# Weight rows moved within 256 bytes, high and low parts interleaved, tokens streamed in either direction

## The chip, the cores and the metric

One NeuronCore of a Trainium2 chip runs the whole program. The metric is the device time of one execution in microseconds. The kernel before was timed twice, and one further execution was taken by the hardware profiler.

## What is computed

One layer of a decoder on 256 prompt tokens and 8 sample tokens, with everything in fp32. The bulk of the arithmetic is matrix products of the 264 tokens with weights; `D_MODEL` is 2048 and the feed-forward width is 5632:

```python
xn = rmsnorm(x, g_mix)
z = xn @ w_in                                   # all inputs of the two mixers
...
x = x + jnp.concatenate([y_rg, y_ml], axis=-1) @ w_out
xq = (rmsnorm(x, g_xa) @ w_xa_q).reshape(B, L, XA_HEADS, XA_DH)
s = jnp.einsum('blhd,bmhd->bhlm', xq, mk.astype(dt)).astype(jnp.float32) * (XA_DH ** -0.5)
...
x = x + o @ w_xa_o
xf = rmsnorm(x, g_ffn)
x = x + (jax.nn.silu(xf @ w_ffn_gate) * (xf @ w_ffn_up)) @ w_ffn_down
```

Between them stand an RG-LRU recurrence, an mLSTM, and attention to 256 memory tokens, whose keys and values (`w_xa_k`, `w_xa_v`) are projected from `mem_prompt`.

## The kernel before

Activations lie with features on the 128 partitions and the 264 tokens along the row. The program is a list, `steps`, written out in order: 41 of `w_in`, 16 of `w_out`, 16 of `w_q`, 32 of `w_k` and `w_v` by turns of four, 16 of `w_o`, then the feed-forward part as three parts of gate, up and down. One step makes one block of 128 output features (or, for `w_v`, adds to a block of 512). Its weights, up to 128x2048, come as two halves of 128x1024 into `raw` (`load_piece`, five buffers, issued by SyncE).

To keep fp32 precision at the fast matmul rate every operand is split into a high and a low part, both of type `float32r`: ScalarE copies the high part out, VectorE subtracts it from the original for the low part. `mm3` then makes three matmuls of each chunk of 128 input features: high by high, high by low, low by high. An ordinary step of 16 chunks so has 48 matmuls. Each loads 128x128 weights as the stationary operand and streams 264 columns of tokens as the moving one, and all 48 add into one PSUM bank.

`split_half` splits the weights of step `i + 1` while step `i` is on TensorE, into `w` tiles (four buffers of 128x2176 elements). In an ordinary step a chunk takes a row of 264 elements there, 128 high and 128 low ones one behind the other, and unused room; `wrows` cuts the rows out, beginning at element `WO`:

```python
WO, WW = 48, 8 * N + 64
...
w = w[:, WO: WO + 8 * N].rearrange("p (c n) -> p c n", n=N)
return w[:, :, 0: P], w[:, :, P: 2 * P]
```

A row of 264 elements is 1056 bytes, so each chunk begins 32 bytes further on, counted modulo 256. The token tiles (`HL`, `Arr`) have the same pitch of 264 elements, four chunks to a tile, and odd tiles begin 32 elements in, so the tokens' chunks move on by 32 bytes in the same way. All `w` and `B` buffers begin at a multiple of 256 bytes. With `WO = 48`, weights and tokens of one chunk therefore always stand 192 bytes apart modulo 256.

The steps of `w_k` and `w_v` are called `wide`: their halves lie in one piece each, the high part at element 0 and the low part at 1088 (both at byte 0 modulo 256). In `w_k` (`pe_k`) the weights are stationary and 512 or 256 token columns move; in `w_v` (`pe_v`) the tokens are stationary and 512 weight columns move. `proj` makes the ordinary steps but for those of `w_o` (`pe_o`), the gates (`pe_if`) and the first four steps (`pe_first`). The first four take their chunks in another order, four outputs at once.

Side work (the recurrences, the norms, attention) runs from generators that `pump` advances between steps within time that the program estimates for ScalarE and VectorE.

Of the kernel before, what the change touches and what calls it, by code (L numbers as in the profile page):

```python
# [17 lines left out]
P = 128  # L18
# [4 lines left out]
N = T + NS  # L23
# [57 lines left out]
def layer_kernel(ctx: ExitStack, tc, xT, memT, vec, wrg, w_in, w_out, w_q, w_k, w_v, w_o,  # L81
# [18 lines left out]
    def nm(s):  # L100
        uid[0] += 1
        return f"{s}_{uid[0]}"
# [16 lines left out]
    WO, WW = 48, 8 * N + 64  # L119
# [29 lines left out]
    steps = []  # L149
    LD, LS = 3, 1  # L150

    raws, splits, wide = {}, {}, set()
# [15 lines left out]
    def split_half(i, h):  # L168
        if i >= len(steps):
            return  # L170
        if steps[i][2] is pe_if:
            if h == 0:
                split_gates(i)
            return
        if i < 4:
            split_first(i, h)
            return
        nch = min(8, steps[i][1] // P - 8 * h)
        w = sb.tile([P, WW], F32R, tag="w", bufs=4, name=nm("w"))
        if i in wide:  # L180
            wh, wl = w[:, 0: 1024], w[:, 1088: 2112]
            with tc.high_priority():
                act.activation(wh, raws[i][h], AF.Copy)
                dve.tensor_sub(wl, raws[i][h], wh.bitcast(F32))
            splits[i, h] = (wh, wl)
            return
        wh, wl = wrows(w, i)
        r = raws[i][h].rearrange("p (c m) -> p c m", m=P)
        with tc.high_priority():
            st["split"] = act.activation(wh[:, :nch], r[:, :nch], AF.Copy)  # L190
            dve.tensor_sub(wl[:, :nch], r[:, :nch], wh[:, :nch].bitcast(F32))
        splits[i, h] = (wh, wl)
# [9 lines left out]
    def split_first(i, h):  # L202

        wh, wl = wrows(sb.tile([P, WW], F32R, tag="w", bufs=4, name=nm("w")), i)
        r = raws[i][h].rearrange("p (c m) -> p c m", m=P)
        with tc.high_priority(), in_order():
            for c in range(2):
                x, k = 4 * i + 2 * h + c, slice(4 * c, 4 * c + 4)
                split(*xn(x), xres[:, x, :], V("g_mix", x))
                st["split"] = act.activation(wh[:, k], r[:, k], AF.Copy)  # L210
                dve.tensor_sub(wl[:, k], r[:, k], wh[:, k].bitcast(F32))
        splits[i, h] = (wh, wl)

    def wrows(w, i):

        w = w[:, WO: WO + 8 * N].rearrange("p (c n) -> p c n", n=N)
        return w[:, :, 0: P], w[:, :, P: 2 * P]

    class W:
        def __init__(self, i):  # L220
# [11 lines left out]
    def mm3(ps, a, b, start, stop):  # L232
        ah, al = a
        bh, bl = b
        pe.matmul(ps, ah, bh, start=start, stop=False)
        pe.matmul(ps, ah, bl, start=False, stop=False)
        pe.matmul(ps, al, bh, start=False, stop=stop)
# [50 lines left out]
    def bank(tag="mm"):  # L288
        return psm.tile([P, 512], F32, tag=tag, bufs=4, name=nm(tag))
# [266 lines left out]
    def split_gates(i):  # L556

        for h in range(2):
            w = wrows(sb.tile([P, WW], F32R, tag="w", bufs=4, name=nm("w")), i)[0]
            x = raws[i][h].rearrange("p (c m) -> p c m", m=P)  # L560
            with tc.high_priority():
                act.activation(w[:, :, 0:64], x[:, :, 0:64], AF.Copy)
                dve.tensor_sub(w[:, :, 64:128], x[:, :, 0:64], w[:, :, 0:64].bitcast(F32))
            splits[i, h] = w
# [303 lines left out]
    def proj(src, rhs, evac, cols=2048, n=N, need=()):  # L868

        def f(i):  # L870
            ps = bank()
            w = W(i)
            nch = cols // P
            for c in range(nch):
                mm3(ps[:, :n], w(c), rhs(c), c == 0, c == nch - 1)
            return ps
        steps.append((src, cols, f, evac, need))

# [411 lines left out]
    with tc.high_priority(), in_order():  # L1290
        act.dma_start(vecs[:, 0:16], vec[:, 0:16])
        load_x(act, 1, 2)
        load_x(act, 2, 4)
        act.activation(warm_act, ones[:, 0:1], AF.Square)
        split_half(0, 0)
        split_half(0, 1)

    pend = []
    for i, (src, cols, pef, evf, need) in enumerate(steps):
# [13 lines left out]
        now = pe.clock  # L1313
        dve.clock, act.clock = max(dve.clock, now), max(act.clock, now)
        split_half(i + LS, 0)
        if i + LS < len(steps) and steps[i + LS][1] > 1024:
            split_half(i + LS, 1)
        ps = pef(i)
# [133 lines left out]
```

## Time and profile before

| | us |
|---|---|
| timed runs | 1550.17 and 1552.97, median 1551.57 |
| span of the profiled execution | 1548.1 |
| what lies around the span, by the two timed runs | 2.1 to 4.9 |
| TensorE, matmuls busy | 1533.5 (99%) |
| TensorE, weight loads busy | 1500.4 (97%) |
| VectorE busy | 1055.5 (68%) |
| ScalarE busy | 784.0 (51%) |
| GpSimd busy | 123.7 (8%) |
| mean DMA rate over the span | 211 GB/s |

PE is TensorE's matmul side and PEld its weight loads, which run beside the matmuls. Matmuls are pipelined: a row's duration is longer than the distance from its start to the next one's start, and it is the distance that adds up to the span. Nearly all engine work is issued through one helper, line 60, so the groups tell instructions apart by the tiles that they write and read: `mm<-B,w` are projection matmuls (token tiles `B`, weights `w`), `w<-raw` the splitting of weights.

### The profile page before, as it was taken

The numbers are of one execution on the slowest core, as the hardware profiler recorded it, in microseconds if no ns is written. First come the engines' busy times: TensorE is split into PE (matmuls) and PEld (weight loads), VectorE is DVE, ScalarE is ACT, GpSimd is POOL, SyncE is SP. The second block draws the span as 40 slices with busy tenths as digits, with TensorE's granted clock in tenths as the row PEclk, the third lists the DMA queues.
The fourth block names the chain that finished last, engine by engine and source line by source line (L and its number), as shares of the span: only waits on it lengthen the run. The fifth ranks groups of instructions, "written<-read, shape, count | busy, mean of one in ns | idle before, by whom it ended". The sixth has DMA issues, their size and how long they took to land.

```text
span 1548.1 us, 30188 instructions
## 1 busy us (share of the span) xinstructions
PE 1533.5 (99%) x12098; PEld 1500.4 (97%) x12098; DVE 1055.5 (68%) x2026; ACT 784.0 (51%) x1255; POOL 123.7 (8%) x190
## 2 busy tenths in 40 slices
PE   9999999999999999999999999999999999999997
PEld 9999999999999888899999999999999999999997
DVE  7886888796699989876665555445555545555554
ACT  7565775665455656555444444333444433444463
POOL 0001210000134333310000000000000000000000
PEclk9999999999999999999999999999999999999999
DMA  9556984547789887855555555555555555555563
GB/s 301 187 164 204 309 288 171 193 158 259 251 294 356 320 296 252 309 181 180 187 177 181 186 181 188 181 185 183 183 185 181 186 183 186 180 188 178 163 181 107
DMA packets 99757, 326.01 MB, mean 211 GB/s; under 512 B 10945, under 2 KB 19825, under 8 KB 99617
## 3 DMA queue, kind: packets, MB, share of 16 engines
q1 hardware_dynamic: 83472, 269.57, 52.1%
q0 software_dynamic: 15136, 53.16, 9.7%
q8 instruction: 94, 1.54, 0.4%
q10 hardware_dynamic: 1008, 1.36, 0.3%
q14 instruction: 47, 0.38, 0.1%
HBM read 312.78 MB, written 11.28 MB: 209 GB/s over the span
## 4 chain that ended last, share of the span: by engine, by line
PE 96%; DVE 2%; ACT 1%; DMA 0%; issue 0%; SPq 0%; DVEq 0%; ACTq 0%
PE mm L60 90%; PE ax L60 6%; DVE B L60 1%; ACT B L60 0%; DVE w L60 0%; DMA raw<-w_in 0%; ACT w L60 0%; ACT L60 0%; DVE xres L60 0%; DVE c L60 0%; ACT rstd L60 0%; SPq L1278 0%; DVE acc_x L60 0%; DVEq L1429 0%; ACT t L60 0%
## 5 line engine op out<-in xcount | busy, mean ns | idle before, releaser
L60 PE MATMUL mm<-B,w 128*128 128x264 f32 (+1 forms) x10960 | 1365.3, 285 | 4.1 <-DVE w L60 2.4
L60 PEld LDWEIGHTS mm<-B,w 128*128 128x128 f32 x10960 | 1338.6, 188 | 16.4 <-DVE w L60 2.8
L60 ACT ACTIVATE w<-raw 128x1024 fp32r<-128x1024 f32 (+1 forms) x522 | 537.9, 1031 | 654.6 <-PE mm L60 447.3
L60 DVE TENSOR_TENSOR w<-raw,w 128x1024 fp32r<-128x1024 f32 (+1 forms) x522 | 623.1, 1195 | 357.0 <-ACT w L60 356.0
L60 PE MATMUL mm<-w,B 128*128 128x512 f32 x384 | 91.0, 391 | 0.0
L60 PEld LDWEIGHTS mm<-w,B 128*128 128x128 f32 x384 | 70.7, 188 | 14.3
L60 DVE TENSOR_TENSOR t<-mm,rstd 128x264 f32<-128x264 f32 x104 | 44.8, 431 | 44.2 <-PE mm L60 43.5
L1344 POOL TENSOR_TENSOR B<-B,rstd 128x264 f32<-128x264 f32 x4 | 2.8, 736 | 855.5 <-ACT rstd L60 855.5
L60 DVE TENSOR_TENSOR xres<-xres,mm 128x264 f32<-128x264 f32 (+1 forms) x81 | 34.2, 423 | 38.9 <-PE mm L60 38.9
L60 DVE SCALAR_TENSOR_TENSOR B<-B,dw 128x256 f32<-128x256 f32 x128 | 55.6, 488 | 3.9 <-ACT dw L60 3.9
L60 DVE SCALAR_TENSOR_TENSOR dw<-B,qsm,dw 128x256 f32<-128x256 f32 x96 | 49.6, 525 | 0.4
L60 PE MATMUL ax<-B,B 128*128 128x256 f32 (+3 forms) x288 | 48.1, 308 | 0.0
L60 PEld LDWEIGHTS ax<-B,B 128*128 128x128 f32 x288 | 40.8, 190 | 3.2 <-ACT w L60 0.3
L1031 POOL TENSOR_TENSOR ds<-dw,ds 128x256 fp32r<-128x256 f32 x32 | 34.6, 1085 | 108.1 <-ACT ds L60 108.1
L60 ACT ACTIVATE B<-xres,vecs 128x264 fp32r<-128x264 f32 (+1 forms) x64 | 32.1, 502 | 1.5 <-DVE xres L60 1.0
L60 ACT ACTIVATE t<-xres 128x264 f32<-128x264 f32 (+2 forms) x61 | 24.0, 410 | 15.2 <-DVE xres L60 15.2
L1020 POOL DMA_DIRECT2D B<-kcT x32 | 17.3, 542 | 140.1 <-DVE B L60 131.0
L60 ACT ACTIVATE B<-t 128x264 fp32r<-128x264 f32 (+1 forms) x60 | 24.2, 409 | 4.6 <-DVE t L60 4.3
L60 DVE TENSOR_TENSOR acc_x<-acc_x,t 128x264 f32<-128x264 f32 x59 | 25.1, 426 | 1.0 <-ACT t L60 0.5
L60 DVE SCALAR_TENSOR_TENSOR B<-xres,vecs,B 128x264 fp32r<-128x264 f32 x48 | 23.4, 487 | 3.1 <-ACT B L60 3.1
L60 ACT ACTIVATE t<-t 128x264 f32<-128x264 f32 (+1 forms) x61 | 24.8, 406 | 1.3 <-DVE t L60 1.2
L60 ACT ACTIVATE dw<-B,qsm 128x256 f32<-128x256 f32 x32 | 16.2, 507 | 17.4 <-DVE B L60 10.7
(152 smaller groups left out, 666.9 us busy)
## 6 DMA issues: line engine op xcount, KB each, us to landing
raw<-w_gu SPq DMA_DIRECT2D x176, 512.0 KB, 3.5
raw<-w_d SPq DMA_DIRECT2D x80, 512.0 KB, 3.5
raw<-w_in SPq DMA_DIRECT2D x74, 512.0 KB, 4.6
raw<-w_out SPq DMA_DIRECT2D x32, 512.0 KB, 4.0
B<-kcT POOLq DMA_DIRECT2D x32, 512.0 KB, 8.1
raw<-w_q SPq DMA_DIRECT2D x32, 512.0 KB, 3.7
B<-vcT POOLq DMA_DIRECT2D x32, 512.0 KB, 8.5
raw<-w_k SPq DMA_DIRECT2D x32, 512.0 KB, 6.8
```

What stands on the lines that cost most here:

```text
L60: return f(*a, **k)
L1020: pool_e.dma_start(kc, kcT[h, b])
L1031: pool_e.tensor_sub(ws[:, 1], acc, ws[:, 0].bitcast(F32))
L1344: e.tensor_mul(st["y"](c), st["y"](c), r)
```

## The change

The place of the weights, their layout and the direction of the token stream become functions of the step. `placed(i)` gives three values for an ordinary step that is the `j`-th of its kind, counted from step 4 without the gates and the wide steps: the first element, `4 * (j // 4 % 16)`, which is a multiple of 16 bytes from 0 to 240; whether the high and low parts lie side by side (odd `j`); and whether the tokens are streamed backwards (`j % 4` of 2 or 3). The first four steps and the gates keep what they had.

Side by side means that element `2m` of a row is the high part of weight `m` and element `2m + 1` its low part, so ScalarE and VectorE write, and TensorE loads, with a step of two elements. Backwards means that the moving operand and the PSUM output are both read and written from the last column to the first, which leaves each token's sum at its own place. `pe_o` takes place and layout from `wrows` but always streams forwards. In the wide steps the first element becomes `4 * ((i - 4) % 16)`.

```diff
         w = sb.tile([P, WW], F32R, tag="w", bufs=4, name=nm("w"))
         if i in wide:
-            wh, wl = w[:, 0: 1024], w[:, 1088: 2112]
+            o = 4 * ((i - 4) % 16)
+            wh, wl = w[:, o: o + 1024], w[:, 1088 + o: 2112 + o]
...
     def wrows(w, i):
 
-        w = w[:, WO: WO + 8 * N].rearrange("p (c n) -> p c n", n=N)
+        o, side_by_side, _ = placed(i)
+        w = w[:, o: o + 8 * N].rearrange("p (c n) -> p c n", n=N)
+        if side_by_side:
+            w = w[:, :, 0: 2 * P].rearrange("p c (m j) -> p c j m", j=2)
+            return w[:, :, 0], w[:, :, 1]
         return w[:, :, 0: P], w[:, :, P: 2 * P]
+
+    def placed(i):
+
+        if i < 4 or steps[i][2] is pe_if:
+            return WO, False, False
+        j = len([k for k in range(4, i) if k not in wide and steps[k][2] is not pe_if])
+        return 4 * (j // 4 % 16), j % 2 == 1, j % 4 > 1
...
             ps = bank()
             w = W(i)
             nch = cols // P
+            back = slice(None, None, -1 if placed(i)[2] else 1)
             for c in range(nch):
-                mm3(ps[:, :n], w(c), rhs(c), c == 0, c == nch - 1)
+                mm3(ps[:, :n][:, back], w(c), [v[:, back] for v in rhs(c)], c == 0, c == nch - 1)
             return ps
```

## The prediction

> **What bounds the kernel now.** I read the busy shares and the forty slices first, then the chain that ended last.
>
> ```profile
> span 1548.1 us, 30188 instructions
> PE 1533.5 (99%) x12098; PEld 1500.4 (97%) x12098; DVE 1055.5 (68%) x2026; ACT 784.0 (51%) x1255; POOL 123.7 (8%) x190
> ...
> PE   9999999999999999999999999999999999999997
> ...
> PEclk9999999999999999999999999999999999999999
> ...
> PE 96%; DVE 2%; ACT 1%; DMA 0%; issue 0%; SPq 0%; DVEq 0%; ACTq 0%
> PE mm L60 90%; PE ax L60 6%; DVE B L60 1%; ACT B L60 0%; DVE w L60 0%; DMA raw<-w_in 0%; ACT w L60 0%; ACT L60 0%; DVE xres L60 0%; DVE c L60 0%; ACT rstd L60 0%; SPq L1278 0%; DVE acc_x L60 0%; DVEq L1429 0%; ACT t L60 0%
> ```
>
> TensorE is the bound from the first slice to the last, at full granted clock, and 90% of the chain is the projection matmuls. So the time is the number of matmuls times the distance from one start to the next; anything else is worth only what it adds to that distance. The groups, shapes kept apart:
>
> ```profile
> L60 PEld LDWEIGHTS mm<-B,w 128*128 128x128 f32 x10960 | 1338.6, 188 | 16.4 <-DVE w L60 2.8 <-ACT cso L60 1.9
> L60 PE MATMUL mm<-B,w 128*128 128x264 f32 x10448 | 1272.4, 283 | 4.1 <-DVE w L60 2.4 <-DVE B L60 1.7
> ```
>
> One weight load per matmul, nearly no idle time. A row's mean of 283 ns is latency, not rate; the rate comes from windows without idle time (matmuls that were in flight at an edge have to be taken off the counts). In order: the first four steps, two stretches of the `w_k` steps, the `w_v` steps, and the feed-forward steps.
>
> ```profile
> core 0: us, PE busy (x), PEclk, DMA share, GB/s
> 7.60:30.40 22.80, 22.80 (x190) 1.00 1.00 334
> 481.15:492.12 10.97, 10.97 (x65) 1.00 0.88 300
> 578.65:588.42 9.77, 9.77 (x57) 1.00 0.95 344
> 650.63:665.39 14.76, 14.76 (x68) 1.00 0.52 172
> 1000.00:1143.70 143.70, 143.70 (x1203) 1.00 0.55 184
> ```
>
> - Feed-forward, 264 tokens wide: about 1200 starts in 143.70 us, **119.75 ns** each.
> - `w_v`, 512 wide: 65 in 14.76 us, 227.1 ns, or 0.4435 ns a column. At that rate 264 columns are **117.1 ns**: the distance contains 2.65 ns that streaming alone does not explain.
> - `w_k`, 512 and 256 wide by turns: 63 in 10.97 us is 174.1 ns, 55 in 9.77 us is 177.6 ns. Their mean width is 386 columns, 171.2 ns at 0.4435, so the surplus is 2.9 ns in one stretch and 6.4 in the other, with the same addresses within 256 bytes.
> - The first four steps, 264 wide: 188 in 22.80 us, **121.3 ns**, a surplus of 4.2. In these steps alone the order of the chunks makes the weights' place minus the tokens' place (modulo 256 bytes) pass through all multiples of 32; in the later 264-wide steps with split weights it is always 192.
>
> The other stream is the weight load. Where the tokens are one column wide, only the loads are left:
>
> ```profile
> 39.74 0.75 PEld L60 LDWEIGHTS ax<-ones,acc_x 128*128 128x128 f32 x6
> 39.85 0.72 PE L60 MATMUL ax<-ones,acc_x 128*128 128x1 f32 x6
> 40.41 0.19 PEld L60 LDWEIGHTS mm<-B,w 128*128 128x128 f32 x1
> ```
>
> Six loads from 39.74 to 40.41 are **112 ns** each, 5 ns under the 117.1 of the stream that covers them. So two streams of nearly equal length run beside each other, and the surplus is what they lose to each other or to their phase. That is what the change touches.
>
> **The change part by part.** Instructions, order, waits, DMAs, queues and buffers are the same in both built programs; only addresses and steps inside operands differ. Of the 264-wide matmuls 10368 change: 2784 read packed weights with tokens forwards, 2784 side-by-side weights (step 2) forwards, 2400 packed weights backwards, 2400 both. Sixteen places in steps of 16 bytes are passed through in turn.
>
> *Place, all 10368, and the `w_k`/`w_v` steps.* Now 2.65 ns of surplus at one relative place. Bounds: 0 (all surplus gone, -2.65 ns) and the worst stretch of `w_k` (6.4, so +3.75). The nearest row is the first four steps, which mix the relative places as the change will: 4.2, so +1.6 ns. For the packed half, 5184 x 1.6 = +8.3 us (bounds -13.7 and +19.4). The wide steps already wander between 2.9 and 6.4 ns at one place, so I take 0 for their 512 `w_k` matmuls (bounds -1.5 and +1.8 us).
>
> *Side by side, 5184 matmuls.* The load of one set then spans 1024 bytes instead of 512. No row shows a strided load. From below: the load stays 112 ns and loses the surplus, -2.65 ns (-13.7 us). From above: each load takes twice as long since it covers twice the bytes, 224 ns, which becomes the distance: 224 - 119.75 = +104 ns (+540 us). Between them, `w_v`'s tokens show that TensorE takes 2048 bytes in 227.1 ns, so 1024 bytes in 113.5: a load at that rate is still under 117.1, but the slack falls from 5.1 to 3.6 ns and the load meets the token stream over twice the bytes. I take the first steps' 1.6 plus as much again for the second half of the bytes, +3.2 ns: 5184 x 3.2 = +16.6 us.
>
> *Backwards, 4800 matmuls.* Tokens and PSUM columns run with step -1; no row shows it. From below, the surplus goes: -2.65 ns, -12.7 us. From above, one half of the rate: 117 ns more, +562 us. The lengths of both streams are unchanged, so I take 0.
>
> *Making the weights.* ScalarE and VectorE now write, and VectorE also reads, with step 2 in every second of these steps.
>
> ```profile
> L60 DVE TENSOR_TENSOR w<-raw,w 128x1024 fp32r<-128x1024 f32 x50 | 61.2, 1225 | 52.8 <-ACT w L60 52.8
> L60 ACT ACTIVATE w<-raw 128x1024 fp32r<-128x1024 f32 x50 | 53.0, 1061 | 86.0 <-PE mm L60 63.5 <-issue 22.6
> ```
>
> These rows are of the 143.70 us window. ScalarE waits 63.5 us there for TensorE to free a `w` buffer: weights are made ahead, and the next load waits for nothing. Cost nothing; cover is TensorE's own 5.75 us a step (48 x 119.75). Were the strided halves twice as slow, VectorE would gain 2 x 1.225 = 2.45 us in every second step, 30.6 us in this window, and the 52.8 us that it waits ahead of its `w` rows hold that. Without that cover, 2.3 us a half (1.061 + 1.225) would come ahead of the step's matmuls.
>
> *Sum.* +8.3 + 16.6 + 0 + 0 = +24.9 us on 1548.1 of span. The two timed runs are 1550.17 and 1552.97 (median 1551.57, 3.5 above the span), so I forecast **1576 us**, 1.6% more.
>
> **The rivals.**
>
> *A, forecast: the surplus grows by a few ns.* For it: the first steps, where mixed places cost 1.6 ns. Against: the second half of its price is an analogy between the token stream and the load. Its own range is 1551 to 1605.
>
> *B, the strided load becomes the bound but isn't doubled.* The slack is only 5 ns, so a load of 140 ns sets the distance: +20 x 5184 = +104 us, 1655 us. It decides from about 118 ns a load. For it: the load has almost no slack now. Against: 113.5 ns at the stream's rate. Range 1600 to 1690.
>
> *C, backwards runs at half rate.* Distance 234 ns in 4800 matmuls: 1551.6 + 562 + 25 = 2138 us. For it: no forward row excludes it. Against: the bytes are contiguous in either direction and arrive in the same runs. The Trainium skill, "PSUM — Partial Sum Buffer", Specifications (TRN2), says that PSUM is organised in lines of 8 bytes and that any access pattern that isn't contiguous slows matmuls significantly; if a step of -1 counts as that, C is what it would do here, and no run here shows yet whether it counts.
>
> *D, the strided load takes twice as long.* +104 x 5184 = +540, 2092 us (with places, 2100). For it: nothing but the absence of a row. Against: the `w_v` tokens' rate. The Trainium skill, "SBUF — State Buffer", Specifications (TRN2), states that full bandwidth needs at least two hits in each 16-byte line; step 2 in fp32 leaves just two, so by it D does not happen. No trace here shows this either way.
>
> *E, faster: the two streams stop disturbing each other.* Side by side, load and tokens cover their bytes at nearly one rate (1024 bytes in 112 to 113.5 ns against 1056 in 117.1), so at most places they might keep apart, and another direction may keep the phase. Its most is the surplus of all: 10368 x 2.65 = 27.5 us, 1524; half of it, 1538 us. It decides from where the mean distance falls below 119.75 ns. For it: the phases in `w_k` that differ by 3.5 ns at one address. Against: places mixed in the first steps were slower.
>
> *F, nothing changes:* the surplus is the phase alone, and the means come out alike, 1551. The places are really moved in the built program, so this is the seam between A and E and shares their chances.
>
> **How the numbers follow.** A 0.47 (0.37 up to 1582.6, 0.10 above), B 0.20, C 0.13, D 0.05, E 0.15 (0.03 of it over 2%). A change of 2% (31 us) is about what a measurement of this kernel can tell from none. Faster: 0.03. Within: 0.37 of A and 0.12 of E, 0.49. Slower: 0.10 + 0.20 + 0.13 + 0.05 = 0.48. The range leaves out C, D and the far end of E, 0.20 together, and reaches from 1530 to the end of B, 1690.
>
> **What would show it.** Starts in windows of the feed-forward steps. Packed forwards near 121.3 ns, side by side near 123, backwards like forwards: A. Side-by-side steps above 130 while packed ones stay: B; near 224: D. Backward steps near 234 whatever the weights: C. All below 119.75: E. TensorE should stay at 99% with idle time as now; if it waits for `w`, the making of weights was mispriced. VectorE's `w` mean over 1300 ns would show the strided halves slower, yet hidden. I am wrong if any of the four combinations stands more than 10 ns from the others.

## The result and the profile after

The changed kernel took 1571.08 us (median of 1570.49 and 1571.66) against 1551.57: 1.0124 times the time before, 95% interval 1.0094 to 1.0153, so it is slower by 19.5 us, or 1.2%. The interval leaves out 1, though the change is under 2%. The forecast was 1576 us, with 1.6%.

The page of the changed kernel, and its groups with the shapes kept apart:

```profile
span 1568.7 us, 30182 instructions
PE 1554.3 (99%) x12098; PEld 1519.9 (97%) x12098; DVE 1056.1 (67%) x2026; ACT 806.4 (51%) x1255; POOL 125.4 (8%) x190
```

```profile
L60 PE MATMUL mm<-B,w 128*128 128x264 f32 x10448 | 1291.8, 285 | 3.7 <-DVE w L60 2.0 <-DVE B L60 1.7
L60 DVE TENSOR_TENSOR w<-raw,w 128x1024 fp32r<-128x1024 f32 x488 | 599.4, 1229 | 376.8 <-ACT w L60 375.9
L60 ACT ACTIVATE w<-raw 128x1024 fp32r<-128x1024 f32 x488 | 539.8, 1107 | 648.6 <-PE mm L60 437.4 <-issue 191.0 <-ACT B L60 10.0
```

The span grew by 20.6 us and TensorE's busy time by 20.8. 264-wide matmuls grew by 19.4 us at the same count and nearly the same idle time, so the distance between starts grew. VectorE writes side-by-side weights as fast as packed ones (a mean of 1229 ns for 1230). ScalarE's mean grew by 47 ns, from 1060: 212 of its 488 halves are side by side, and those take 1168 ns, the others 1060 as before. It still waits for TensorE 437 us in all.

Since the change makes four consecutive steps of the four kinds at each place, its own trace can be read as a survey. Windows of the changed kernel, cut at the starts of steps: the four at place 192 (packed, side by side, packed backwards, both), one packed forward step at place 128, and the whole feed-forward part; then that part before:

```profile
core 0: us, PE busy (x), PEclk, DMA share, GB/s
948.64:954.39 5.75, 5.75 (x50) 1.00 0.53 185
954.39:960.30 5.91, 5.91 (x50) 1.00 0.52 177
960.30:966.18 5.88, 5.88 (x50) 1.00 0.51 179
966.18:971.96 5.78, 5.78 (x51) 1.00 0.52 182
855.09:861.04 5.95, 5.95 (x51) 1.00 0.52 179
783.79:1550.84 767.05, 767.05 (x6314) 1.00 0.51 177
```

```profile
774.52:1530.25 755.73, 755.73 (x6314) 1.00 0.54 180
```

A step has 48 matmuls (two or three in each count began earlier), so the first four rows are 119.8, 123.1, 122.5 and 120.4 ns a matmul and the fifth is 124.0. The feed-forward part of 6336 matmuls grew by 11.3 us, 1.79 ns each. Taken apart by start times of single matmuls, the means over its places, against 119.75, are about +1.7 (packed), +2.6 (side by side), +1.8 (packed backwards) and +1.0 ns (both). The place and kind of the kernel before, 119.75 ns, is the best of the 64 combinations. The rest of the 20.6 us arose in the same way: 6.5 us before the wide steps, 1.4 in them, 1.4 in the steps of `w_o`.

### The profile page after: what moved, and what is told of

It is laid out like the page before. It is cut to its first block, busy times and chain, and to the rows that moved or that the text cites. A ratio compares the mean times of both kernels' runs of the same rounds, so it can differ in the third digit from the quotient of the medians.

```text
span 1568.7 us, 30182 instructions
## 1 busy us (share of the span) xinstructions
PE 1554.3 (99%) x12098; PEld 1519.9 (97%) x12098; DVE 1056.1 (67%) x2026; ACT 806.4 (51%) x1255; POOL 125.4 (8%) x190
## 4 chain that ended last, share of the span: by engine, by line
PE 96%; DVE 2%; ACT 1%; DMA 0%; issue 0%; SPq 0%; DVEq 0%; ACTq 0%
PE mm L60 90%; PE ax L60 6%; DVE B L60 2%; DVE w L60 0%; ACT B L60 0%; DMA raw<-w_in 0%; ACT w L60 0%; ACT L60 0%; DVE xres L60 0%; DVE c L60 0%; ACT rstd L60 0%; SPq L1291 0%; DVEq L1442 0%; DVE acc_x L60 0%; DVE t L60 0%
## 5 line engine op out<-in xcount | busy, mean ns | idle before, releaser
L60 PE MATMUL mm<-B,w 128*128 128x264 f32 (+1 forms) x10960 | 1384.2, 288 | 3.7 <-DVE w L60 2.0
L60 PEld LDWEIGHTS mm<-B,w 128*128 128x128 f32 x10960 | 1358.2, 192 | 15.6 <-DVE w L60 2.5
L60 ACT ACTIVATE w<-raw 128x1024 fp32r<-128x1024 f32 (+1 forms) x522 | 561.6, 1077 | 662.5 <-PE mm L60 447.8
```

What stands on the lines that cost most here:

```text
L60: return f(*a, **k)
```

## The experiments

**One part at a time.** Four kernels, each with one part of the change. In `placed`:

```diff
-        return 4 * (j // 4 % 16), j % 2 == 1, j % 4 > 1
+        return 4 * (j // 4 % 16), False, False    # place alone
+        return WO, True, False                    # side by side alone
+        return WO, False, True                    # backwards alone
+        return WO, True, True                     # both at the old place
```

The wide steps are as before in all four, and the steps of `w_o` in the last three.

> Only the place moves, through 16 places with 16 bytes between them, packed and forwards in every ordinary step; the wide steps as before. Theory (the distance between matmuls depends only on where and how the load and the token stream of neighbouring matmuls lie): the packed forward steps of the changed kernel have a mean of 121.45 ns, so 10368 x 1.7 = +18 us, 1569 to 1570. Rival (the steps before decide, by the phase they leave): no mean carries over, between 1552 and 1580. Rival (the strided writing of weights cost the time): no change, 1552.

Measured 1568.56 us, 1.011 (1.0095 to 1.0125). The mean came out nearly as the theory has it: +16.6 us over 10368 matmuls, 1.60 ns each for 1.7. Taken place by place in the feed-forward steps, 13 of the 16 places keep the distance that they had in the changed kernel within half a ns, and three (112, 128 and 208) don't.

> Only side by side, at the old place 192, forwards; the steps of w_o and the wide ones as before, so 9600 matmuls change. Theory: the one such place in the changed kernel showed 123.1 ns, so 9600 x 3.35 = +32 us, 1584. Rival (phase of earlier steps): anything from 120.3 to 124 ns, 1557 to 1592. Rival (writers): also slower, and then the fourth kernel is as slow as this one.

Measured 1580.45 us, 1.0185 (1.017 to 1.02), 4 us under the theory's 1584.

> Only the direction: packed, at the old place 192, backwards in the same 9600 matmuls. Theory: 122.5 ns as in the changed kernel's steps of this kind, +26 us, 1578. Rival (phase): 120.3 to 122.5 ns, 1557 to 1578. Rival (writers): 1552, since nothing is written with a step.

Measured 1577.43 us, 1.0165 (1.0148 to 1.0182), as the theory has it.

> Side by side and backwards together, at the old place, in the same 9600 matmuls. Theory: 120.3 ns, +5 us, 1557, although each alone costs 26 to 32. Rival (phase): 120.3 to 122.5 ns, 1557 to 1578. Rival (writers): as slow as side by side alone. If the costs of the two simply added: +58 us, 1610.

Measured 1557.2 us, 1.004 (1.0025 to 1.0054), again as the theory has it. The same window of the feed-forward steps in the four kernels, in this order:

```profile
1000.00:1300.00 300.00, 300.00 (x2474) 1.00 0.54 181
```
```profile
1000.00:1300.00 300.00, 300.00 (x2451) 1.00 0.54 180
```
```profile
1000.00:1300.00 300.00, 300.00 (x2452) 1.00 0.54 180
```
```profile
1000.00:1300.00 300.00, 300.00 (x2497) 1.00 0.55 183
```

With two or three taken off each count: 121.4, 122.5, 122.5 and 120.3 ns. Step 2 in the weights costs 2.8 ns at the old place, backwards costs 2.8, and both together 0.5, so the parts do not add. That rules out the writers: the fourth kernel writes with a step as the second does. Phase is not ruled out. Side by side at place 192 was 123.1 in the changed kernel and 122.5 here, and the packed forward step at place 128 (124.0 above) is in the kernel with the place alone:

```profile
853.93:859.71 5.78, 5.78 (x51) 1.00 0.57 184
```

120.4 ns. The same addresses have at least two rhythms. One difference beside the steps before remains in this pair: in the changed kernel the next step's weights are written side by side meanwhile, here packed. The next experiment has the same step of the changed kernel, with side-by-side writing beside it (one ScalarE half of 1.16 us), but behind matmuls 512 columns wide:

```profile
972.46:978.26 5.80, 5.80 (x50) 1.00 0.56 175
```

That is 120.7 ns by the starts, so the writing alone doesn't make the slow rhythm: what ran just before can choose between the two. How it does so isn't shown. In the changed kernel the step's first six matmuls still lie 120.7 ns apart, and from the twenty-first on 124.8.

**The load and the stream by themselves.** Added matmuls whose results nothing reads, after the gate and up steps of the changed kernel:

```diff
+                for c in range(nch):
+                    for k in range(2):
+                        pe.matmul(scr[:, 0:8], w(c)[k], rhs(c)[0][:, 0:8], start=True, stop=True)
+                for c in range(nch):
+                    t = st["ffn"].h.tile(c // 4).rearrange("p c n -> p (c n)")[:, 0:512]
+                    pe.matmul(scr[:, back], w(c)[0], t[:, back], start=True, stop=True)
```

> The changed kernel with added matmuls after each gate and up step, into a bank that nothing reads: 32 matmuls only 8 columns wide, so that the distance is the weight load alone, packed or side by side and at the step's place; then 16 matmuls 512 columns wide in the step's direction, so that the distance is the token stream with a load that ends long before it. Theory (the surplus arises between the two streams, neither is longer by itself): load alone 112 ns packed and 112 to 114 side by side, stream 227 ns forwards and backwards. Rival (the strided load is itself the bound): 118 to 123 ns side by side. Rival (streaming backwards is itself slower): 232 ns or more backwards.

Windows within two runs of 8-column matmuls, packed and side by side:

```profile
853.00:855.60 2.60, 2.60 (x25) 1.00 0.00 0
931.20:934.20 3.00, 3.00 (x28) 1.00 0.00 0
```

By the starts inside them, 23 and 26, that is 112 ns packed and 117 side by side. Over the 21 or 22 runs of each kind, as far as they ran at full clock, the means are 111.7 and 117.4. This lies between theory and rival: the strided load does get longer, to just under what the stream takes. Within or after most of these runs the clock halved for a while: the 512-wide matmuls then took 426 to 427 ns, and the clock granted over the span was 0.90. At full clock they took about 232 ns forwards and 234 backwards, both more than the theory's 227, so the direction alone is not what makes backwards dear.

**One address instead of a row.** Again after the gate and up steps, four runs of 24 matmuls: as in the step, weights from one address, tokens from one address, both.

```diff
+                        if kind & 1:
+                            ww = [x[:, 0:1].to_broadcast([P, P]) for x in ww]
+                        if kind & 2:
+                            vv = [v[:, 0:1].to_broadcast([P, n]) for v in vv]
```

> The changed kernel with four added runs of 24 matmuls after each gate and up step, into a bank that nothing reads: as in the step; with weights that all come from one address (step 0); with tokens that all come from one address; with both. The products of these runs mean nothing. Theory (both streams compete for parts of the row memory that their places select): as in the step 120 to 124 ns; weights from one address: the surplus mostly gone, 117 to 118 at every place; tokens from one address: no competition, bound by the load or by 264 columns, 110 to 113; both: the same 110 to 113. Rival (the surplus is a matter of phase between two clocked streams and not of places): 120 ns or more with weights from one address too.

Windows of these four runs after a packed forward step, and after a side-by-side forward one, both at place 96:

```profile
859.45:862.40 2.95, 2.95 (x26) 1.00 0.02 7
862.40:865.29 2.89, 2.89 (x26) 1.00 0.53 181
865.29:867.99 2.70, 2.70 (x26) 1.00 0.00 0
867.99:870.69 2.70, 2.70 (x26) 1.00 0.00 0
876.55:879.46 2.91, 2.91 (x26) 1.00 0.01 6
879.46:882.36 2.90, 2.90 (x27) 1.00 0.51 181
882.36:885.18 2.82, 2.82 (x26) 1.00 0.00 0
885.18:887.88 2.70, 2.70 (x26) 1.00 0.00 0
```

Divided by 24: 122.9, 120.4, 112.5, 112.5; then 121.3, 120.8, 117.5, 112.5. Tokens from one address remove everything, whatever the place of packed weights; side by side then shows its load of 117. Weights from one address do **not** bring the distance to 117: it stays at 120.2 to 121.6 at every place and in every kind. Here the theory fell. A 264-column token stream takes 120.3 ns or more here with a load that reads one address only; real weights, in steps without a wait, give 119.7 to 124.8, which is -0.6 to +4.5 ns against that. The PSUM writes are the same in all four runs, so at 112.5 ns they are no limit. That one address costs the stream nothing isn't shown.

**The stream by width and start.** In the kernel before, added runs of 24 matmuls with one repeated stream, with weights from one address and with the step's packed ones:

```diff
+                    if g % 2 == 0:
+                        x = x[:, 0:1].to_broadcast([P, P])
+                    pe.matmul(scr[:, :width], x, t[:, s: s + width], start=True, stop=True)
```

> The kernel before with added runs of 24 matmuls after 72 of the gate and up steps, into a bank that nothing reads; each variant twice, with weights that all come from one address and with the step's packed weights at place 192. Token streams 264 wide from 16 starts with 16 bytes between them; from one start with widths of 232 to 512; and 264 wide with three starts by turns, 1024 to 1152 bytes apart. The products mean nothing. Theory (a stream pays for each 256 bytes that it crosses): all starts alike but for the last one (five crossings for four), 117 ns there and less elsewhere, and the distance grows in jumps with the width. Rival (each stream is fitted into a fixed rhythm of the memory, so that a matmul's distance is rounded up by what its end misses): distances at 264 columns stay at 120 whatever the start, and go up and down against a straight line with the width, with widths that are multiples of 64 on the line of 0.4435 ns a column. If weights at one address give the same as packed ones in a repeated stream, the load takes no part.

Timeline rows: 264 columns from element 8 and weights from one address; 256 columns from element 0, likewise; 256 with packed weights.

```profile
821.31 3.04 PE L60 MATMUL ax<-B,w 128*128 128x264 f32 x24
824.20 0.40 PE L60 MATMUL mm<-B,w 128*128 128x264 f32 x2
```
```profile
1206.17 2.91 PE L60 MATMUL ax<-B,w 128*128 128x256 f32 x24
1208.92 0.29 PE L60 MATMUL mm<-B,w 128*128 128x264 f32 x1
1214.68 3.00 PE L60 MATMUL ax<-B,w 128*128 128x256 f32 x24
1217.52 0.28 PE L60 MATMUL mm<-B,w 128*128 128x264 f32 x1
```

From one start to the next group's: 2.89 us for 24 is 120.4 ns, 2.75 is 114.6, 2.84 is 118.3. Without the edges the means are about 120.2, 113.6 and 118.4. Weights from one address make a jump behind 256 columns: four more (260) cost 6 ns at once (119.7). With packed weights there is none to speak of (118.4, then 120.2), so here the load takes part. And 320, 384 and 512 are not on the line of 0.4435 ns a column either, with weights from one address (146.4, 173.8, 231.8 for 141.9, 170.3, 227.1), so the fixed rhythm fits the jump at most and not the rest. The theory of crossings fell too: starts differ (118.3 to 120.3), and the one with five crossings was among the two cheapest.

**The wide steps alone.** The kernel before with the change's place in the wide steps:

> The kernel before with the place of the wide steps' weights alone moved as in the change. Theory (place of load against stream): as in the changed kernel, the w_v steps go from 228 to 233 ns and the w_k steps lose half a ns a matmul, +1.5 us in all, 1550 to 1557 in time. Rival (phase left by the ordinary steps): the w_v steps stay at 228.

1553.23 us in one run beside 1553.14 for the kernel before. The groups of the 512-wide `w_v` matmuls, before and in this kernel:

```profile
L60 PE MATMUL mm<-w,B 128*128 128x512 f32 x384 | 91.0, 391 | 0.0
```
```profile
L60 PE MATMUL mm<-w,B 128*128 128x512 f32 x384 | 92.8, 396 | 0.0
```

In the traces the theory held: +1.8 us here (228.1 to 233.0 ns), -0.5 in `w_k`. The two times don't show the 1.3 us, which is less than runs of the kernel before differ among themselves (1550.14 to 1554.42 us).

**Looking for a better place.** Three surveys of the same kind as the change, packed and forwards: places with 4 bytes between them and four orders of the three matmuls; the low token parts 128 bytes away; and token rows that begin at 16 bytes modulo 32. Their edits are one line each beside the return of `placed`, the first with the four orders in `mm3`:

```diff
+        return 40 + j // 4 % 16, False, j % 4      # 4 bytes; the last is the order in mm3
+        return 4 * (j // 4 % 16), False, j % 4     # and Arr: 32 * ((q + self.odd) % 2), odd = 1 in the low parts
+        return j // 2 % 64, False, False           # and Arr: 4 + 24 * (q % 2)
```

> Packed and forwards, with places 160 to 220 in steps of 4 bytes (instead of 16), and the order of the three matmuls of a chunk taken from four by turns: now (high-high, high-low, low-high), high-high low-high high-low, high-low high-high low-high, and now with its mirror image in every second chunk. Theory (places of the load against the stream that it runs beside): all places within one 16-byte step alike or close, 119.8 around 192 for the present order; other orders differ by 0 to 3 ns since other loads run beside other streams; none below 117.1. Rival (phase): 4 bytes change the distance as much as 16 do.

Steps at places 192 and 172, both in the third order:

```profile
865.82:871.57 5.75, 5.75 (x50) 1.00 0.57 183
1123.29:1129.27 5.98, 5.98 (x50) 1.00 0.55 178
```

119.8 and 124.6 ns. At 160, 164, 168 and 172, the distances were 120.3, 122.5, 121.4 and 124.7: 4 bytes matter as much as 16, as the rival said. Place 172 had two rhythms again, 124.7 in the step shown and 122.0 in one of the last, shorter steps. The order of the three matmuls hardly matters (means 121.6 to 121.8).

> Packed and forwards, 16 places with 16 bytes between them, the same four orders, and the tiles of the low token parts 128 bytes away (modulo 256) from those of the high parts. Theory (places): in two of three matmuls nothing moves, in the third the relative place shifts by 128; the distances lie between 118.5 and 124 ns, with the best place no longer 192. Rival (phase): the same spread without order in the places.

The best step here, place 128 in the second order:

```profile
861.32:867.09 5.77, 5.77 (x50) 1.00 0.56 182
```

120.2 ns; the means are 121.4 to 121.8, without a visible order in the places.

> Packed, forwards and in the old order, with the token tiles moved so that every token row begins at 16 bytes modulo 32 (instead of 0), and with the weights at 64 places with 4 bytes between them, two steps at each. Theory (the token stream by itself is the larger part, and rows at 16 modulo 32 were cheaper when repeated with weights from one address, 118.4 to 120.3 with a mean of 119.3, against 119.7 to 120.3): the mean over places falls from 121.4 to 120.5, and the best places lie at 118.5 to 119.3, under the 119.75 of the kernel before. Rival (a repeated stream says nothing of a sequence of rows): mean 121.4 as before and none under 119.7.

The best step here, place 196:

```profile
865.44:871.19 5.75, 5.75 (x50) 1.00 0.56 183
```

119.8 ns, and the mean is 121.5. The rival held: what a repeated row costs says nothing of a sequence of rows. One thing more differs in this survey: odd token tiles now begin 24 elements behind even ones instead of 32, so each step mixes two relative places that lie 32 bytes apart. None of the three surveys shows a combination under 119.7 ns, so none of them points to a version faster than the kernel before.

**What a load pays for its step.** The last run measures the term that the forecast priced by analogy. A stationary operand is read from a token tile with a step of 0 to 8 elements, with 8 columns moving, then 264:

```diff
+                x = t[:, 0: 128 * step: step] if step else t[:, 0:1].to_broadcast([P, P])
+                for k in range(24):
+                    m = rhs(4 + k % 4)[0]
+                    pe.matmul(scr[:, :264 if wide_ else 8], x, m if wide_ else m[:, 0:8], start=True, stop=True)
```

> The kernel before with added runs of 24 matmuls after 36 of the gate and up steps, into a bank that nothing reads; the stationary operand is read from a token tile with steps of 0 to 8 elements, first with 8 columns moving (the load alone) and then with 264. The products mean nothing. Theory (a strided load is priced by the 16-byte pieces that it reads, one piece as long as the token stream takes for one, 1.77 to 1.83 ns): 112 ns at steps 0 and 1, 117 at step 2 (64 pieces), 165 to 175 at step 3 (96 pieces), 227 to 235 at step 4 and the same at 5 to 8 (128 pieces), and with 264 columns the larger of this and 120 ns. Rival (by the bytes that it spans): 117 at step 2 and a growth with every further step up to 450 at step 8. Rival (the step costs a fixed 5 ns): 117 at all steps from 2 on.

Timeline rows with 8 columns, steps 1, 2, 3 and 4, each with the matmuls that follow:

```profile
801.93 2.74 PE L60 MATMUL ax<-B,B 128*128 128x8 f32 x24
804.53 0.37 PE L60 MATMUL mm<-B,w 128*128 128x264 f32 x1
```
```profile
821.91 2.88 PE L60 MATMUL ax<-B,B 128*128 128x8 f32 x24
824.64 0.37 PE L60 MATMUL mm<-B,w 128*128 128x264 f32 x1
```
```profile
842.21 4.34 PE L60 MATMUL ax<-B,B 128*128 128x8 f32 x24
846.41 0.57 PE L60 MATMUL mm<-B,w 128*128 128x264 f32 x1
```
```profile
866.53 5.64 PE L60 MATMUL ax<-B,B 128*128 128x8 f32 x24
872.03 0.57 PE L60 MATMUL mm<-B,w 128*128 128x264 f32 x1
```

By 23, since the first is loaded ahead: 113, 119, 183 and 239 ns; away from the edges 111.7, 117.8, 173.7 and 233.3. Steps 5 to 8 stay at 220 to 238, and with 264 columns steps 3 and 4 set the distance at 175 and 235. Windows at step 4, with 8 columns and with 264:

```profile
866.53:872.03 5.50, 5.50 (x26) 0.78 0.57 189
1074.39:1080.00 5.61, 5.61 (x26) 1.00 0.57 185
```

With 8 columns the granted clock fell, to 0.78 here; with 264 it was full, and the distance the same within 2 ns, so these loads don't owe their length to the clock. The theory of 16-byte pieces held within 8 ns; spanned bytes and a fixed cost are both out.

## Why the prediction was right, point by point

*TensorE is the bound and the distance between starts is the whole matter:* right; its busy time grew as the span did.

*Place, +1.6 ns:* right in size. Moved alone it cost 1.60 ns a matmul. The first four steps were a fair sample, although each place has a distance of its own and some have two. They change the place with every chunk and the change with every fourth step, so an agreement this close is in part luck.

*Side by side, +3.2 ns (16.6 us):* too dear. It was +2.6 ns forwards and +1.0 backwards in the feed-forward steps; at these means the 2784 and 2400 matmuls make 9.7 us. Two errors stand behind the term. The load was priced at 113.5 ns and is 117.4. And what that longer load would do was guessed as twice the disturbance, while backwards it disturbs less than a packed one does.

*Backwards, nothing beyond the place:* right on average for packed weights (+1.8 against +1.7 forwards), but the average hides much: at the old place it costs 2.8 ns, and with side-by-side weights it saves 1.6. That the two directions come out alike over the sixteen places is luck as far as the prediction goes; its reason, that both streams keep their lengths, holds at each place alike.

*The wide steps, 0:* measured +1.4 us: +1.8 in `w_v`, whose old place was better than all eight that it was moved to (231 to 234 ns for 228), and -0.5 in `w_k`; only `w_k` had been priced.

*Making the weights, nothing:* right. ScalarE is slower by 108 ns in each side-by-side half (1168 for 1060), hidden.

*The rivals.* The load becomes the bound (B): not at step 2; its condition, 118 ns, was missed by less than 1 ns, and at step 3 it is true (175 ns). Half rate backwards (C) did not happen: 122.5 ns. By the Trainium skill, "PSUM — Partial Sum Buffer", Specifications (TRN2), backward steps would have slowed significantly, if a step of -1 counted as not contiguous; with 120.3 to 122.5 ns backwards at place 192 the trace says that it does not count so. A doubled load (D) did not happen at step 2, with two values in 16 bytes (117.8 ns for 111.7), and did at step 4, with one (233). This agrees with the Trainium skill, "SBUF — State Buffer", Specifications (TRN2), on two hits a line. Faster (E): no single combination of the change went below the 119.75 ns of the kernel before.

*What was wrong in the reading.* The 117.1 ns "of streaming alone" came from 512-wide matmuls and was scaled to 264 columns. A stream of 264 that is read from a row shows no such rate in any run: with weights that all come from one address it takes 120.3 ns. So nothing shows that the surplus of 2.65 ns was what load and stream lose to each other, and the price of E, 27.5 us, had no ground. The forecast did not hang on it, since its terms were differences between measured distances; the story around them did.

What stays open: why 264 columns take 120.3 ns where 256 take 113.6, both with weights from one address, why place 192 is faster than such weights, and by what a step falls into one of two rhythms. None of the runs shows the memory's own clock.

## What to carry to other kernels

Price a change of layout by the distance between starts in windows that TensorE fills, and look for steps in the old trace that already have the new addresses: here such a sample was right to a tenth of a nanosecond, an analogy with another stream was not. A rate does not scale from one width to another, so measure each width. When a kernel repeats one step some hundred times, letting a layout vary from step to step makes one profile a survey of all of them; but then judge the steps and not the total, and run the chosen ones alone, since a step can inherit its neighbour's rhythm.

## What the runs showed of the hardware

- A matmul with 264 `float32r` columns takes 112.5 ns if all columns come from one address, and 118.3 to 121.6 ns if they come from a row and the weights from one address. 256 columns then take 113.6, and 118.4 with packed weights.
- Loading 128x128 weights takes 112 ns at steps 0 and 1, 117 to 118 at step 2, 174 at step 3 and 220 to 238 at steps 4 to 8.
- The place of weight rows modulo 256 bytes changes the distance of the same matmuls from 119.7 to 124.7 ns, and 4 bytes can make 1 to 3 ns. One set of addresses can have two distances (120.4 and 124.0 ns at place 128), by what ran before.
- Streaming tokens and writing PSUM from the last column to the first costs from -2.9 to +2.8 ns of 120 with packed weights, by the place; with step-2 weights it gives nearly the same 120.3 ns at 13 of 16 places.
- Most runs of 32 matmuls only 8 columns wide were followed by matmuls at half clock (427 ns for 512 columns, which take 232 at full clock).
